# Which engine subtracts the low parts of the down projection's weight blocks: GpSimd or DVE

## The chip, the cores and the metric

One core of one Trainium2 chip runs the whole layer in one launch. The metric is the device time of that launch in microseconds; lower is better. The engines are called as the profile calls them: PE (TensorE), DVE (VectorE), ACT (ScalarE), POOL (GpSimd) and SP, whose queue issues nearly all DMAs.

## The reference, cut to what matters

The layer is a token mixer (Fourier groups and gated DeltaNet heads) followed by a gated convolutional feed-forward, all in float32, for 1024 tokens of width 1024 and a hidden width of 2816. The change lies in the last matrix product of the second part:

```python
def conv_ffn(h, w_up_l, w_dwc_l, w_down_l, on_grid):
    p = h @ w_up_l
    val, gate = p[..., :D_FF], p[..., D_FF:]
    gate = lax.conv_general_dilated(gate.reshape(bsz, rows, GRID_W, D_FF), w_dwc_l[:, :, None, :], ...)
    return (jax.nn.silu(gate) * val) @ w_down_l          # 1024 x 2816 times 2816 x 1024
...
xl = xl + gt2l * rmsnorm(conv_ffn(hl, ...), g_post_ffn[i])
```

## The kernel before, in words

**Split products.** A float32 operand is split into a high part that PE multiplies exactly and a low part that is what is left: high = cast (ACT), low = full minus high (`sub_l`, L164 and L165). `mm3` (L189 to L193) then makes each product of three matmuls: high by high, high by low, low by high. L191 to L193 are the lines of nearly every matmul in the profile, and L165 is the line of every low-part subtraction, whichever engine does it.

**The down projection.** It is the last stage of the kernel (the loop from L1774). The product is cut into 2 x 2 x 2 blocks and done with seven block products instead of eight, so there are seven passes (`PASSES`, L1552), each of 11 steps (`NJ`): 77 steps, numbered n = 0 to 76. A step multiplies four tiles of 128 tokens with one weight block of 128 x 512, which is 4 x 3 = 12 matmuls. A pass collects in four PSUM banks. In passes 0 to 3 either the activations or the weights are a sum of two blocks; in passes 4, 5 and 6 both are.

**What one step needs** is made by `prep(n)` (L1576 to L1608):
- the weight block, one or two DMAs from SP into `raw` (L1589; a page `pg` or, for every fourth step, one of two buffers named `wr`), and for two blocks their sum on DVE (L1591);
- its high part `wh` (cast on ACT, L1598) and its low part `wl` (L1599, shown under L165), each in a ring of four buffers; the last six steps take pages (`pg`) instead;
- the activations: their sum on DVE (L1603, into `s` or one of four halves of `pad`), the cast on ACT (L1606) and the low part on DVE (L1607, shown under L165 as pg<-pad,pg or pg<-pg,pg).

`prep(n + 5)` is written while step n multiplies, so work is prepared up to five steps ahead; the four buffers of `wh` and `wl` let step n's block be split only once PE is done with step n - 4. `raw` is free for its next load when its last reader, the subtraction of `wl`, is done; the DMAs that fill it stand in SP's queue, in order.

```python
nc.scalar.copy(wh, raw[:, 0])
self.sub_l(nc.gpsimd, wl, raw[:, 0], wh)
...
gs = self.page2()
nc.scalar.copy(gs[:, 0], src[0])
self.sub_l(V, gs[:, 1], src[0], gs[:, 0])
```

**What else runs there.** When a pass ends, ACT copies its four banks out (L1804), and small jobs are put into the list `late`, one of which is taken out per step: sums of pass results on POOL (L1808, L1812, L1818, L1820, all shown under L1448), the square and scaling of a finished half (`early`, L1737), and the output of four token tiles (`out`, L1743 to L1757), where DVE does the small norm arithmetic (L201 to L206, L1751) and the last multiply-add (L1756). The last six steps of pass 6 are done tile by tile (L1792), each tile followed by its `out`. The steps 0 to 3 are prepared while the up projection still runs (L1722); DVE is then busy with the taps of the depthwise convolution (L1471), after which ACT applies SiLU (L1475).

The order of the instructions on each engine is fixed when the program is built, by a scheduler that follows the data; each engine then takes its own list strictly in order.

Of the kernel before, what the change touches and what calls it, by code (L numbers as in the profile page):

```python
# [100 lines left out]
class Kern:  # L101
# [1323 lines left out]
    def ffn(self):  # L1425
        nc, tc, A = self.nc, self.tc, self.A
        V = nc.vector
        wu = A["w_up"][0].rearrange("(k p) n -> p k n", p=P)
        with tc.tile_pool(name="ffn", bufs=1, reuse_waits="tile") as fp:
# [134 lines left out]
            def gpart(f, i):  # L1564

                if f not in here:
                    here[f] = [f >= NF - 5] * 2
                    if not here[f][0]:
                        g[f] = self.pg()
                c = slice(512 * i, 512 * i + 512)  # L1570
                if not here[f][i]:
                    nc.sync.dma_start(g[f][:, c], gd[f][:, c])
                    here[f][i] = True
                return g[f][:, c]

            def prep(n):  # L1576

                ps, j = divmod(n, NJ)
                ga, wa = PASSES[ps]
                if ps == 4 and j == 0:  # L1580
                    self.gp2 = self.pg()
                    nc.sync.dma_start(self.gp2, self.gp[1])
                if n % 4:
                    raw = self.pg().rearrange("p (a n) -> p a n", a=2)
                else:
                    raw = self.wp.tile([P, 2, 512], F32, tag="raw", bufs=2, name=self.nm("wr"))
                for x, (k, c, _) in enumerate(wa):
                    f = j + NJ * k
                    nc.sync.dma_start(raw[:, x], A["w_down"][0, f * P:(f + 1) * P, 512 * c:512 * c + 512])  # L1589
                if len(wa) > 1:  # L1590
                    V.tensor_tensor(raw[:, 0], raw[:, 0], raw[:, 1], op=ALU.add if wa[1][2] > 0 else ALU.subtract)  # L1591
                if ps == 6 and j >= NJ - 6:
                    hl = self.page2()
                    wh, wl = hl[:, 0], hl[:, 1]
                else:
                    wh = self.wp.tile([P, 512], F32R, tag="wh", bufs=4, name=self.nm("wh"))
                    wl = self.wp.tile([P, 512], F32R, tag="wl", bufs=4, name=self.nm("wl"))
                nc.scalar.copy(wh, raw[:, 0])  # L1598
                self.sub_l(nc.gpsimd, wl, raw[:, 0], wh)  # L1599
                src = [gpart(j + NJ * k, i) for i, k, _ in ga]  # L1600
                if len(ga) > 1:
                    tmp = big("s") if ps == 0 else tmps[n % 4]
                    V.tensor_tensor(tmp, src[0], src[1], op=ALU.add if ga[1][2] > 0 else ALU.subtract)  # L1603
                    src = [tmp]
# [3 lines that stand above are left out]
                return gs, wh, wl  # L1608
# [74 lines left out]
            for n, (f, p) in enumerate(seq):  # L1683
# [38 lines left out]
                if n >= len(seq) - 4:  # L1722
                    i = len(ops)
                    ops[i] = prep(i)
            work(len(back))
            for i in range(5):
                if i not in ops:
                    ops[i] = prep(i)
# [45 lines left out]
            for ps in range(7):  # L1774
                bk = banks[BSET[ps]]
                for j in range(NJ):
                    n = ps * NJ + j
                    a = 5
                    if ps == 6 and j >= 5:
                        a += j - 5 + 1  # L1780
                    for i in range(n + 5, min(n + a, NS - 1) + 1):
                        if i not in ops:
                            ops[i] = prep(i)
                    if n < NS - 6:
                        for t in range(4):
                            mm(n, t)
                    if late and j > 0 and (ps < 6 or len(late) > 4 or j % 5 == 5 - 1):
                        late.pop(0)()
                    if ps in (5, 6) and j >= NJ - 5 and len(ahead) < 4 * (ps - 4):
                        load_x1(len(ahead))  # L1790
# [69 lines left out]
```

## Time and profile before

| what | value |
| --- | --- |
| time, median of 3 runs | 1411.86 us (1411.44 to 1413.65) |
| time of the profiled execution | 1411.65 us |
| its span, first to last instruction | 1409.9 us |
| mean granted TensorE clock | 0.978 |
| busy share of PE / DVE / ACT / POOL | 92% / 74% / 44% / 48% |
| down projection, from its first matmul | about 1142.6 us to the end |

Times in the profile count from the start of the span. A duration of PE is modelled at its end, so the pace of matmuls is read from the distance between starts. "Idle before" is time in which the engine had nothing to do before the instruction, with the engine and line that ended the wait. On DVE neighbouring instructions overlap by some 0.08 us, so there too the distance between starts is the cost.

### The profile page before, as it was taken

To read this page: it belongs to the slowest core of one execution; us is meant where nothing else is said; L and a number is where in the kernel's file an instruction comes from. 1 tells how busy PE (TensorE), PEld (TensorE's weight loads), DVE (VectorE), ACT (ScalarE), POOL (GpSimd) and SP (SyncE) were. 2 spreads that over 40 slices of the span, in tenths; PEclk is the share of its full clock that TensorE was granted. 3 is DMA by queue.
4 is the path that set the end of the run, shared out by engine and by line. 5 is a ranking of instruction groups with operands and counts; after the bars stand their busy time and mean duration, and the time that the engine had idled before them with its cause. 6 is when DMAs were issued, how large, how long until landed. Compare 5 with 4: busy or idle time off the path is not lost.

```text
span 1409.9 us, 19321 instructions
## 1 busy us (share of the span) xinstructions
PE 1296.7 (92%) x6678; PEld 1028.1 (73%) x6678; DVE 1044.1 (74%) x1715; ACT 614.2 (44%) x1292; POOL 675.5 (48%) x593
## 2 busy tenths in 40 slices
PE   5999999989899999989988999999999989998685
PEld 2677876566566889877866777888888877886564
DVE  3675556836855847865688888888887899799977
ACT  5343456433543234345354344444444445454432
POOL 0440123232351354345365666666666647656773
PEclk9999999999999999999999999999999999999988
DMA  9522237676386778542403133222332285443454
GB/s 326 175 97 82 69 90 219 206 202 210 137 235 226 256 237 268 182 143 86 156 21 87 63 90 90 76 90 75 90 90 75 78 268 192 162 142 122 141 209 179
DMA packets 181427, 209.47 MB, mean 149 GB/s; under 512 B 31383, under 2 KB 119505, under 8 KB 181329
## 3 DMA queue, kind: packets, MB, share of 16 engines
q1 hardware_dynamic: 180465, 205.09, 45.2%
q0 software_dynamic: 864, 3.15, 0.7%
q8 instruction: 53, 0.87, 0.2%
q14 instruction: 45, 0.37, 0.1%
HBM read 161.01 MB, written 47.19 MB: 148 GB/s over the span
## 4 chain that ended last, share of the span: by engine, by line
PE 43%; DVE 17%; DMA 5%; issue 5%; POOL 5%; ACT 3%; SPq 0%; DVEq 0%; ACTq 0%; POOLq 0%
PE ps L191 11%; PE ps L192 11%; PE ps L193 11%; PE ps L1081 3%; POOL wl L165 2%; DVE cv L1471 2%; DVE pg L165 2%; PE ps L1025 1%; DVE T L982 1%; DVE s L1448 1%; POOL pg L165 1%; DVE pg L984 1%; PE ps L305 1%; DVE pg L1756 1%; POOL pg L1006 1%
## 5 line engine op out<-in xcount | busy, mean ns | idle before, releaser
L191 PE MATMUL ps<-pg,wh 128*128 128x512 f32 (+1 forms) x896 | 352.8, 394 | 13.2 <-ACT m L1703 10.0
L193 PE MATMUL ps<-pg,wl 128*128 128x512 f32 (+1 forms) x896 | 348.2, 389 | 0.6 <-POOL wl L165 0.6
L192 PE MATMUL ps<-pg,wh 128*128 128x512 f32 (+1 forms) x896 | 347.6, 388 | 0.0
L1471 DVE SCALAR_TENSOR_TENSOR cv<-pad,dw,cv 128x1024 f32<-128x1024 f32 x176 | 226.4, 1286 | 16.5 <-ACT cv L1469 13.1
L191 PEld LDWEIGHTS ps<-pg,wh 128*128 128x128 f32 x896 | 170.0, 190 | 62.9 <-issue 15.0
L165 POOL TENSOR_TENSOR wl<-wr,wh 128x512 fp32r<-128x512 f32 x86 | 126.2, 1472 | 179.8 <-ACT wh L183 123.7
L193 PEld LDWEIGHTS ps<-pg,wl 128*128 128x128 f32 x896 | 170.7, 190 | 37.1 <-issue 3.5
L192 PEld LDWEIGHTS ps<-pg,wh 128*128 128x128 f32 x896 | 170.7, 190 | 31.2 <-issue 0.4
L165 POOL TENSOR_TENSOR wl<-pg,wh 128x512 fp32r<-128x512 f32 x83 | 124.1, 1499 | 98.7 <-ACT wh L1641 54.1
L165 POOL TENSOR_TENSOR wl<-s,wh 128x512 fp32r<-128x512 f32 x80 | 107.4, 1344 | 54.0 <-ACT wh L1641 53.5
L192 PE MATMUL ps<-wl,pg 128*128 128x512 f32 x250 | 101.7, 407 | 22.0 <-POOL wl L165 21.9
L191 PE MATMUL ps<-wh,pg 128*128 128x512 f32 x250 | 101.0, 405 | 6.2 <-ACT pg L1606 3.5
L1641 ACT CAST wh<-s 128x512 fp32r<-128x512 f32 x80 | 49.6, 621 | 121.5 <-PE ps L192 109.5
L193 PE MATMUL ps<-wh,pg 128*128 128x512 f32 x250 | 99.6, 400 | 0.0
L193 PE MATMUL ps<-pg,pg 128*128 128x512 f32 (+1 forms) x248 | 96.7, 392 | 2.9 <-POOL pg L165 2.1
L191 PE MATMUL ps<-pg,pg 128*128 128x512 f32 (+1 forms) x248 | 97.5, 393 | 0.8 <-DVE pg L476 0.8
L192 PE MATMUL ps<-pg,pg 128*128 128x512 f32 (+1 forms) x248 | 96.4, 389 | 1.4 <-POOL pg L165 1.4
L192 PEld LDWEIGHTS ps<-wl,pg 128*128 128x128 f32 x250 | 48.5, 194 | 35.7 <-POOL wl L165 26.1
L191 PEld LDWEIGHTS ps<-wh,pg 128*128 128x128 f32 x250 | 48.6, 195 | 17.7 <-ACT pg L1606 4.0
L1081 PE MATMUL ps<-pg,pg 128*128 128x128 f32 x464 | 58.4, 277 | 2.7 <-DVE pg L1143 1.8
L1081 PEld LDWEIGHTS ps<-pg,pg 128*128 128x128 f32 x464 | 54.8, 192 | 4.6 <-DVE pg L1143 2.2
L193 PEld LDWEIGHTS ps<-pg,pg 128*128 128x128 f32 x248 | 47.0, 190 | 15.2 <-POOL pg L165 3.6
(363 smaller groups left out, 2540.5 us busy)
## 6 DMA issues: line engine op xcount, KB each, us to landing
pg<-in_w_down_dram SPq DMA_DIRECT2D x97, 256.0 KB, 4.5
wr<-in_w_ada_dram SPq DMA_DIRECT2D x32, 512.0 KB, 4.4
wr<-in_w_up_dram SPq DMA_DIRECT2D x24, 512.0 KB, 3.8
wr<-in_w_in_dram SPq DMA_DIRECT2D x20, 512.0 KB, 4.7
pg<-in_w_up_dram SPq DMA_DIRECT2D x20, 512.0 KB, 5.9
wr<-in_w_down_dram SPq DMA_DIRECT2D x35, 256.0 KB, 2.7
gd<-pg SPq DMA_DIRECT2D x17, 512.0 KB, 2.6
pg<-gd SPq DMA_DIRECT2D x34, 256.0 KB, 4.2
```

The lines of the kernel that those rows point to most:

```text
L165: eng.tensor_tensor(l, full, h.bitcast(F32), op=ALU.subtract)
L191: nc.tensor.matmul(out, ah, bh, start=start, stop=False, **kw)
L192: nc.tensor.matmul(out, ah, bl, start=False, stop=False, **kw)
L193: nc.tensor.matmul(out, al, bh, start=False, stop=stop, **kw)
L305: nc.tensor.matmul(ps[32 * j:32 * j + 32, :], self.csil[:, k, :], t[:, a, :], start=(k < 4), stop=(k >= 4), skip_group_check=True, tile_po ...
L982: V.tensor_tensor(tmp, L[:nl, j + 1:, j:j + 1].broadcast_to([nl, r, c]), X[:nl, j:j + 1, 0:c].broadcast_to([nl, r, c]), op=ALU.mult)
L984: V.tensor_tensor(X[:nl, j + 1:, 0:c], X[:nl, j + 1:, 0:c], tmp, op=ALU.subtract)
L1006: nc.gpsimd.tensor_tensor(dst[:, d].rearrange("p h (b c) -> p h b c", b=4), src.unsqueeze(2).broadcast_to([P, H, 4, 32]), mask, op=ALU.mult)
L1025: nc.tensor.matmul(ps[po, h * n:(h + 1) * n], Q[k0:k0 + kn, d, h, po], R[k0:k0 + kn, d, h, c0:c0 + n], start=True, stop=True, skip_group_c ...
L1081: nc.tensor.matmul(ps[:, hs(h)], lhs(h), rhs(h), start=True, stop=True, skip_group_check=True)
L1471: V.scalar_tensor_tensor(c3, src, w, c3, op0=ALU.mult, op1=ALU.add)
L1641: nc.scalar.copy(h, src)
```

## The change

The low part of each of the 77 weight blocks of the down projection is subtracted by DVE. Operands, buffers and loads stay as they are.

```diff
--- before.py
+++ after.py
@@ -1596,7 +1596,7 @@
                     wh = self.wp.tile([P, 512], F32R, tag="wh", bufs=4, name=self.nm("wh"))
                     wl = self.wp.tile([P, 512], F32R, tag="wl", bufs=4, name=self.nm("wl"))
                 nc.scalar.copy(wh, raw[:, 0])
-                self.sub_l(nc.gpsimd, wl, raw[:, 0], wh)
+                self.sub_l(V, wl, raw[:, 0], wh)
                 src = [gpart(j + NJ * k, i) for i, k, _ in ga]
                 if len(ga) > 1:
                     tmp = big("s") if ps == 0 else tmps[n % 4]
```

It changes the lists of two engines most: DVE has 1506 entries instead of 1429, POOL 485 instead of 563 (an entry can stand for two equal instructions in a row).

DVE in pass 5, before, around the weight sums of steps 60 and 58 (`wr_11409` and `pg_11355`); L165 here is the low part of activations only:

```order
L1603 TENSOR_TENSOR pad_6493<-pg_9438 128x512
L165 TENSOR_TENSOR pg_11364<-pad_6494,pg_11364 128x512
L1591 TENSOR_TENSOR wr_11409<-wr_11409 128x512
L165 TENSOR_TENSOR pg_11388<-pad_6494,pg_11388 128x512
L1591 TENSOR_TENSOR pg_11355<-pg_11355 128x512
L1603 TENSOR_TENSOR pad_6494<-pg_9590 128x512
L1603 TENSOR_TENSOR pad_6494<-pg_9742 128x512
```

DVE at the same place with the change; `wl_11256` and `wl_11282` are weight low parts of steps 54 and 55:

```order
L165 TENSOR_TENSOR pg_11364<-pad_6494,pg_11364 128x512
L1603 TENSOR_TENSOR pad_6494<-pg_9932 128x512
L165 TENSOR_TENSOR wl_11256<-pg_11251,wh_11255 128x512
L1591 TENSOR_TENSOR pg_11355<-pg_11355 128x512
L165 TENSOR_TENSOR pg_11388<-pad_6494,pg_11388 128x512
L1591 TENSOR_TENSOR wr_11409<-wr_11409 128x512
L165 TENSOR_TENSOR wl_11282<-pg_11277,wh_11281 128x512
L1591 TENSOR_TENSOR pg_11379<-pg_11379 128x512
```

One weight subtraction now stands in each step's share of the list, between the sums for later steps, and those sums wait behind it.

POOL in pass 5 before, from the sums of pass results on:

```order
L1448 TENSOR_TENSOR pg_11403<-pg_11403,pg_10586 128x512 x2
L1448 TENSOR_TENSOR pg_11404<-pg_11404,pg_10587 128x512
L165 TENSOR_TENSOR wl_11360<-pg_11355,wh_11359 128x512
L1448 TENSOR_TENSOR pg_11404<-pg_11404,pg_10587 128x512
L165 TENSOR_TENSOR wl_11384<-pg_11379,wh_11383 128x512
L165 TENSOR_TENSOR wl_11414<-wr_11409,wh_11413 128x512
L165 TENSOR_TENSOR wl_11438<-pg_11433,wh_11437 128x512
```

POOL at the same place with the change:

```order
L1448 TENSOR_TENSOR pg_11403<-pg_11403,pg_10586 128x512 x2
L1448 TENSOR_TENSOR pg_11404<-pg_11404,pg_10587 128x512 x2
L1448 TENSOR_TENSOR pg_11403<-pg_11403,pg_10995 128x512 x2
L1448 TENSOR_TENSOR pg_11404<-pg_11404,pg_10995 128x512
L1448 TENSOR_TENSOR pg_11125<-pg_11125,pg_10995 128x512
```

Only the sums of pass results and the scalings of the output are left on POOL there.

DVE at the start of the stage with the change, in the last taps of the convolution (L1471); the four `wl` are those of steps 1 to 4:

```order
L165 TENSOR_TENSOR wl_9978<-pg_9975,wh_9977 128x512
L1471 SCALAR_TENSOR_TENSOR cv<-pad_6494,dw,cv 128x1024
L165 TENSOR_TENSOR wl_10010<-pg_10007,wh_10009 128x512
L1471 SCALAR_TENSOR_TENSOR cv<-pad_6494,dw,cv 128x1024
L165 TENSOR_TENSOR wl_10035<-pg_10032,wh_10034 128x512
L1471 SCALAR_TENSOR_TENSOR cv<-pad_6494,dw,cv 128x1024
L165 TENSOR_TENSOR pg_10040<-s_10038,pg_10040 128x512
L1471 SCALAR_TENSOR_TENSOR cv<-pad_6494,dw,cv 128x1024
L165 TENSOR_TENSOR wl_10053<-wr_10050,wh_10052 128x512
L1471 SCALAR_TENSOR_TENSOR cv<-pad_6494,dw,cv 128x1024
```

Before, these taps stand with the activations' sums and subtractions alone; the first of the five early weight subtractions, that of step 0, now stands some ten entries further ahead.

## Rows read from the trace of the kernel before

**Rows 1.** Busy time, share of the span and instructions, from the page.
```profile
PE 1296.7 (92%) x6678; PEld 1028.1 (73%) x6678; DVE 1044.1 (74%) x1715; ACT 614.2 (44%) x1292; POOL 675.5 (48%) x593
```

**Rows 2.** Stretches of the down projection: busy time (count) by engine, granted clock.
```profile
core 0: us, PE busy (x) PEld busy (x) DVE busy (x) ACT busy (x) POOL busy (x), PEclk, DMA share, GB/s
1142.50:1170.00 27.50, 22.24 (x90) 17.50 (x89) 26.30 (x30) 13.01 (x24) 15.34 (x8) 0.94 0.66 224
1170.00:1274.00 104.00, 104.00 (x460) 86.11 (x460) 91.38 (x82) 53.33 (x100) 66.79 (x45) 1.00 0.52 169
1274.00:1383.90 109.90, 85.54 (x336) 65.66 (x334) 98.03 (x113) 40.72 (x80) 77.58 (x45) 0.91 0.43 146
1383.90:1409.90 26.00, 12.76 (x55) 10.25 (x55) 20.03 (x48) 4.41 (x15) 7.09 (x5) 0.79 0.59 212
1249.40:1383.90 134.50, 110.14 (x444) 86.05 (x442) 119.76 (x133) 51.70 (x98) 91.81 (x54) 0.92 0.45 153
```

**Rows 3.** Timeline of PE: start, duration, what, idle before and its releaser.
```profile
1159.95 0.80 PE L191 MATMUL ps<-wh,pg 128*128 128x512 f32 x1 [3.53 <-ACT pg L1606]
1166.73 0.50 PE L192 MATMUL ps<-wl,pg 128*128 128x512 f32 x1 [1.73 <-POOL wl L165]
...
1177.31 0.39 PE L191 MATMUL ps<-wh,pg 128*128 128x512 f32 x1
...
1180.03 0.39 PE L191 MATMUL ps<-wh,pg 128*128 128x512 f32 x1
...
1341.08 0.80 PE L192 MATMUL ps<-wl,pg 128*128 128x512 f32 x1 [9.08 <-POOL wl L165]
```

**Rows 4.** PE's waits from 1170 to 1384: for whom, us in total, times, longest.
```profile
PE ps L192 <- POOL wl L165: 20.2, 7, 9.1
PE ps L191 <- ACT wh L1598: 2.6, 1, 2.6
PE ps L192 <- POOL pg L165: 0.7, 2, 0.4
PE ps L193 <- DVE pg L165: 0.7, 1, 0.7
```

**Rows 5.** Timeline of DVE in passes 5 and 6.
```profile
1311.18 1.78 DVE L1591 TENSOR_TENSOR wr<-wr 128x512 f32<-128x512 f32 x1
...
1333.20 0.69 DVE L1603 TENSOR_TENSOR pad<-pg 128x512 f32<-128x512 f32 x1
1333.80 0.69 DVE L1591 TENSOR_TENSOR pg<-pg 128x512 f32<-128x512 f32 x1
...
1348.43 0.69 DVE L1591 TENSOR_TENSOR pg<-pg 128x512 f32<-128x512 f32 x1 [8.52 <-DMA pg<-in_w_down_dram]
...
1383.18 0.68 DVE L165 TENSOR_TENSOR pg<-pad,pg 128x512 fp32r<-128x512 f32 x1
```

**Rows 6.** Timeline of POOL in pass 5.
```profile
1312.38 1.74 POOL L165 TENSOR_TENSOR wl<-wr,wh 128x512 fp32r<-128x512 f32 x1
...
1331.59 9.44 POOL L165 TENSOR_TENSOR wl<-wr,wh 128x512 fp32r<-128x512 f32 x1 [5.60 <-DVE pg L1591]
...
1346.12 1.29 POOL L165 TENSOR_TENSOR wl<-wr,wh 128x512 fp32r<-128x512 f32 x1 [1.40 <-ACT wh L1598]
```

**Rows 7.** The chain that ended last, in order of time, in passes 5 and 6.
```profile
1335.10 5.94 POOL wl L165
...
1344.33 7.94 DMA pg<-in_w_down_dram
```

**Rows 8.** Groups of POOL's instructions, 1249.3 to 1383.9: busy, mean ns, idle before.
```profile
L165 POOL TENSOR_TENSOR wl<-pg,wh 128x512 fp32r<-128x512 f32 x25 | 38.3, 1536 | 16.3 <-ACT wh L1598 15.2 <-issue 1.1
L165 POOL TENSOR_TENSOR wl<-wr,wh 128x512 fp32r<-128x512 f32 x8 | 21.0, 2628 | 12.6 <-ACT wh L1598 5.7 <-DVE pg L1591 5.6 <-issue 1.3
```

**Rows 9.** Groups of DVE's instructions, the same stretch: a small one.
```profile
L203 DVE RECIPROCAL sums<-rsq 128x1 f32<-128x1 f32 x3 | 0.4, 149 | 0.0
```

**Rows 10.** Timeline of ACT at the start of the stage.
```profile
1158.37 1.02 ACT L1475 ACTIVATE pg<-cv 128x1024 f32<-128x1024 f32 x1 [9.45 <-DVE cv L1471]
```

## The prediction

> **What bounds the kernel now.** PE is busy for 92% of the span [rows 1], an average over stages with different limits, so I read the last stage by stretches [rows 2]. First its floor: twelve matmuls, one step, take 1180.03 - 1177.31 = 2.72 us from start to start, 0.227 us each [rows 3]. From 1170 to 1274 (passes 0 to 3) PE is busy all the time at a granted clock of 1.00 [rows 2]: nothing on another engine can shorten that stretch. From 1274 to 1383.9 (passes 4 to 6) 336 matmuls, worth 336 x 0.227 = 76.3 us, take 109.9 us at a clock of 0.91 [rows 2]: 33.6 us are lost. The waits of PE account for 20.2 + 2.6 + 0.7 + 0.7 = 24.2 us of them, 20.2 for POOL's subtraction of `wl`, the instruction that is moved [rows 4]; the other 9.4 us go with the lower clock after such pauses.
>
> Who is late behind POOL? DVE is busy for 119.8 of the 134.5 us from 1249.4, where it takes up the first weight sum of pass 4, to 1383.9, where its last subtraction for the last step ends [rows 2, 5]. But most of that is not its work. Next to each other stand full-size DVE instructions (128x512, two inputs in SBUF) that cost 0.60 us from start to start and others that take 1.78 us; the long ones lie beside a POOL subtraction that takes 1.74 us where an undisturbed one takes 1.29 [rows 5, 6]. The two engines stand in each other's way, by about 1.78 - 0.68 = 1.10 us for DVE at a meeting. Once it goes the other way: a POOL subtraction that starts at 1331.59 ends 9.44 us later, while DVE runs one 0.69 us instruction after another [rows 5, 6]. PE waits 9.08 us for it [rows 3]; its raw buffer comes free late, the chain goes on through the next load (5.94 us of POOL, then 7.94 us of DMA), and DVE then stands idle for 8.52 us [rows 5, 7].
>
> The Trainium skill says of this ("SBUF — State Buffer", section "Who interferes with whom") that a DVE instruction with two SBUF inputs and a GpSimd instruction that reads SBUF take the shared port for a whole instruction each, and that whichever issues second waits until the first finishes. The 1.78 us rows agree [rows 5]; the 9.44 us row does not, since POOL was held for (9.44 - 1.29) / 0.60, some 13, DVE instructions, not one [rows 5, 6]. By the page alone the 8.5 us term below would not be the port's and would stay.
>
> **The change part by part.**
>
> *POOL loses 77 subtractions.* In the stretch from 1249.4, POOL has 54 instructions; 25 + 8 = 33 are subtractions into the `wl` ring [rows 2, 8], and six more are those of the last six steps, so 39 leave and 15 sums and scalings stay. What did the 54 cost DVE? Of its 133 instructions 115 are full-size and 18 of the small norm kind; at 0.61 and 0.15 us [rows 5, 9] they are worth 70.2 + 2.7 = 72.9 us, so 119.8 - 72.9 = 46.9 us are time in POOL's way, 0.87 us for each POOL instruction. Taking 39 away is worth 39 x 0.87 = 33.9 us.
>
> *DVE gets 39 of the 77 in that stretch*, with the same shape as those it has: 39 x 0.61 = 23.8 us. DVE's busy time falls by 33.9 - 23.8 = **10.1 us**.
>
> *The late load goes.* With no `wl` on POOL none can be held up, so the chain that ended in 8.5 us of DVE idleness has no start: **8.5 us**. The other 134.5 - 119.8 - 8.5 = 6.2 us of idle time in the stretch I leave in. The next late thing is DVE itself: its 119.8 - 10.1 = 109.7 us of work for passes 4 to 6 still exceed PE's 33 x 2.72 = 89.8 us, so PE goes on waiting for it now and then.
>
> *Passes 0 to 3.* DVE gets one more 0.61 us instruction per step, with POOL gone from its way. PE has no wait there [rows 2] and a step has 2.72 us for DVE's three; cost 0. If that cover went (a `wl` standing behind a late load in DVE's list), each 2.72 us that DVE stands still beyond the three steps that are prepared would be one step of PE.
>
> *The start.* Five weight subtractions now stand among DVE's last taps, ahead of the SiLU that ACT waits for and behind which the casts for step 4 stand; ACT waits 9.45 us for those taps [rows 10] and PE 3.53 us for the cast [rows 3]. Cost at most 5 x 0.61 = 3.1 us. Against it, three other full-size DVE instructions (two of L1603, one of L1591) move behind the taps in DVE's list, POOL is out of the way, and the 1.73 us that PE waits for `wl` of a later step [rows 3] can go too: gain at most 3.5 + 1.7 = 5.2 us. I take 0, since additions and removals are nearly equal in number.
>
> *SP's queue* issues the same loads; those into `raw` are released by the subtraction on DVE instead of POOL. I cost this at nothing because the subtraction is shorter, and keep the other case as a rival.
>
> *The tail.* From DVE's last subtraction to the end lie 26 us, mostly 55 matmuls and DVE's final multiply-adds [rows 2]. POOL's scalings there stay. The tail moves as a whole; cost 0.
>
> Sum, against the profiled execution's own 1411.65 us (0.2 us under the median of the three runs): 1411.65 - 10.1 - 8.5 = **1393.0 us**. The ends: PE without any loss from 1274 on, and the best start, give 1411.65 - 33.6 - 5.2 = 1372.9 us; only the 10.1 us and the worst start give 1411.65 - 10.1 + 3.1 = 1404.7 us. I stay near the middle, because the ledger of DVE is made of many equal rows, while the floor supposes that DVE is never late again.
>
> **The rivals.**
>
> *PE's floor is reached.* If DVE, freed of POOL, also starts passes 4 to 6 with more work done ahead, all 33.6 us come back: 1378.1 us. For it: DVE's 115 + 39 = 154 full-size instructions at the undisturbed 0.61 us are 93.9 us, hardly more than PE's 89.8. Against it: 15 POOL instructions remain, worth 13 us of DVE by the same 0.87.
>
> *Hidden anyway: the loads set the pace.* If the 8.5 us of idleness and more of its kind come from late loads whoever frees the buffers, DVE's 10.1 us turn into idle time: about 1411.7 us, no change. Against it: the long wait begins at the held-up subtraction [rows 7], and PE's waits are for `wl`, not for DMA [rows 4]. That the change does not do what it says is excluded by DVE's 77 new entries.
>
> *DVE inherits POOL's waits; slower.* POOL waited 15.2 + 5.7 = 20.9 us for ACT's `wh` in that stretch [rows 8], partly because the ring is full until PE finishes a step. On POOL nothing stood behind that wait; in DVE's list the sums and subtractions for later steps do. If DVE stands still as long and the load chain stays, the time is 1411.65 - 10.1 + 20.9 = 1422.5 us. It decides from the point where the inherited waits exceed 10.1 us, or 18.6 us if the load chain goes. Against it: the ring is full only while PE is behind, and from 1274 on it is PE that waits [rows 4].
>
> *DVE is simply full; slower.* If POOL's presence is not what makes the 1.78 us rows, the 39 subtractions only add: 1411.65 + 23.8 = 1435.5 us. Against it: wherever POOL is held up or idle, DVE's rows are 0.69 us [rows 5]. The Trainium skill's page "Perfetto Trace Analysis" (section "Optimizing Scalar/DVE Operations") advises moving work away from a saturated DVE, even to GpSimd, and adds that shifting it between these two might not help as they share a read port; by its first half this rival would hold, and the 0.60 us starts speak for its second.
>
> **How the numbers follow.** Forecast 0.64, PE's floor 0.19, no change 0.07, inherited waits 0.06, a full DVE 0.04. Faster by over 0.2% (2.8 us, about what a measurement of this kernel can tell from no change): 0.64 + 0.19 = 0.83; within it 0.07; slower 0.06 + 0.04 = 0.10. The predicted time is the forecast's, 1393.0 us. The range holds the forecast and the floor with their bounds, from 1374 (the last microsecond of the best start left out) to 1407 us (2 us past the weaker end, towards no change), and leaves out some 0.19.
>
> **What would show it.** In the profile after: DVE's full-size instructions in passes 4 to 6 mostly at 0.6 to 0.7 us, with some 15 meetings left; no PE wait for a POOL line in the steps; DVE's last subtraction near 1365 us; passes 0 to 3 still without a wait of PE; the clock above 0.91. Wrong would be a DVE that waits for ACT's `wh` or for loads with `wl` behind it, PE waiting in passes 0 to 3, or 1.78 us rows where POOL does nothing.

## The result, and the profile after

| | before | after |
| --- | --- | --- |
| time, median (range), 4 runs each (one of before added) | 1411.65 us (1407.52 to 1413.65) | 1390.46 us (1386.4 to 1395.8) |
| time of the profiled execution, its span | 1411.65 us, 1409.9 us | 1392.15 us, 1390.3 us |
| ratio, 95% interval | | 0.9858 [0.9827, 0.9889] |

The change saves 1.4%, 20.0 us of 1411.65 by the ratio. The forecast was 1393.0 us, faster.

The page first: busy time of each engine, its share of the span, its instructions.

```profile
PE 1297.3 (93%) x6673; PEld 1032.7 (74%) x6678; DVE 1019.5 (73%) x1792; ACT 614.6 (44%) x1292; POOL 547.0 (39%) x516
```

DVE has 77 instructions more than before [rows 1] and is busy 24.6 us less. The stretches of the down projection show where that lies. The second begins and ends where the same work does in [rows 2]: 1247.60 is the first weight sum of pass 4, 1365.20 the end of DVE's last subtraction for the last step.

```profile
core 0: us, PE busy (x) PEld busy (x) DVE busy (x) ACT busy (x) POOL busy (x), PEclk, DMA share, GB/s
1170.00:1274.30 104.30, 104.30 (x461) 86.37 (x461) 82.31 (x128) 55.87 (x105) 7.94 (x6) 1.00 0.54 179
...
1247.60:1365.20 117.60, 108.44 (x453) 87.90 (x452) 108.92 (x171) 52.24 (x100) 24.92 (x15) 0.95 0.52 177
...
1274.30:1365.20 90.90, 81.74 (x335) 65.78 (x334) 87.87 (x139) 38.96 (x77) 22.96 (x14) 0.94 0.51 177
1365.20:1390.30 25.10, 13.24 (x53) 10.45 (x51) 19.17 (x48) 4.42 (x15) 7.10 (x5) 0.77 0.61 220
```

Read against [rows 2]: passes 0 to 3 are as they were, PE busy all the time at a clock of 1.00. From 1274.3 on, 335 matmuls at 0.227 us [rows 3] are worth 76.0 of 90.9 us: 14.9 us are lost where 33.6 were, and the clock is 0.94 where it was 0.91. The stretch from pass 4's first sum to DVE's last subtraction shrinks from 134.5 to 117.6 us, by 16.9; it begins 1.8 us earlier, and the tail is 0.9 us shorter. 16.9 + 1.8 + 0.9 = 19.6 us is the whole difference of the spans, 1409.9 - 1390.3.

What is left of PE's waits of over half a microsecond, from the start of the stage on (timeline of PE: start, duration, what, idle before and its releaser):

```profile
1160.25 0.80 PE L191 MATMUL ps<-wh,pg 128*128 128x512 f32 x1 [3.06 <-ACT pg L1606]
...
1291.95 0.50 PE L192 MATMUL ps<-wl,pg 128*128 128x512 f32 x1 [3.20 <-DVE wl L165]
1314.11 0.79 PE L192 MATMUL ps<-wl,pg 128*128 128x512 f32 x1 [3.94 <-DVE wl L165]
...
1362.56 0.51 PE L191 MATMUL ps<-pg,pg 128*128 128x512 f32 x1 [1.94 <-ACT pg L1606]
```

The 9.08 us wait of before and the 1.73 us wait at the start [rows 3] are gone, and no wait of PE here is for POOL. The last three make 9.1 of the 14.9 us; the other 5.7 us are longer matmuls (busy for 81.7 us instead of 76.0), at the clock of 0.94. The two waits for DVE's `wl` stand right behind sums of pass results that POOL still does. This is the first of them on DVE, with POOL's rows at that time:

```profile
1284.27 0.68 DVE L165 TENSOR_TENSOR pg<-pad,pg 128x512 fp32r<-128x512 f32 x1
1286.15 1.78 DVE L1448 TENSOR_TENSOR s<-s,pg 128x512 f32<-128x512 f32 x1 [1.21 <-POOL pg L1448]
1287.85 1.77 DVE L1591 TENSOR_TENSOR wr<-wr 128x512 f32<-128x512 f32 x1
1289.55 1.75 DVE L1603 TENSOR_TENSOR pad<-pg 128x512 f32<-128x512 f32 x1
1291.22 0.68 DVE L165 TENSOR_TENSOR wl<-pg,wh 128x512 fp32r<-128x512 f32 x1
```

```profile
1283.88 3.50 POOL L1448 TENSOR_TENSOR pg<-s,m 128x512 f32<-128x512 f32 x2 [4.90 <-issue]
1287.35 3.40 POOL L1448 TENSOR_TENSOR pg<-pg,pg 128x512 f32<-128x512 f32 x2
```

DVE has three rows of 1.75 to 1.78 us in a line while POOL works through its sums, and rows of 0.68 us before and behind; the `wl` for which PE waits comes right after. Over the whole stretch DVE's subtraction of `wl` is nearly undisturbed (groups: count, busy, mean ns, idle before), and its last subtraction stands where the forecast put it, near 1365:

```profile
L165 DVE TENSOR_TENSOR wl<-pg,wh 128x512 fp32r<-128x512 f32 x25 | 18.7, 748 | 1.5 <-ACT wh L1598 1.4
```

```profile
1364.50 0.68 DVE L165 TENSOR_TENSOR pg<-pad,pg 128x512 fp32r<-128x512 f32 x1
```

### The profile page after: what moved, and what is told of

Same layout as the page of the kernel before. It is cut to its first block, busy times and chain, and to the rows that moved or that the text cites. A ratio compares the mean times of both kernels' runs of the same rounds, so it can differ in the third digit from the quotient of the medians.

```text
span 1390.3 us, 19234 instructions
## 1 busy us (share of the span) xinstructions
PE 1297.3 (93%) x6673; PEld 1032.7 (74%) x6678; DVE 1019.5 (73%) x1792; ACT 614.6 (44%) x1292; POOL 547.0 (39%) x516
## 4 chain that ended last, share of the span: by engine, by line
PE 41%; DVE 19%; DMA 6%; issue 6%; POOL 4%; ACT 2%; SPq 1%; DVEq 0%; POOLq 0%; ACTq 0%
PE ps L191 11%; PE ps L193 11%; PE ps L192 11%; DVE cv L1471 3%; PE ps L1081 2%; DVE pg L165 2%; DVE s L1448 2%; PE ps L1025 1%; DVE T L982 1%; DMA pg<-in_w_down_dram 1%; DVE pg L984 1%; DVE wl L165 1%; POOL wl L165 1%; POOL pg L165 1%; PE ps L305 1%
## 5 line engine op out<-in xcount | busy, mean ns | idle before, releaser
L191 PE MATMUL ps<-pg,wh 128*128 128x512 f32 (+1 forms) x896 | 353.1, 394 | 12.8 <-ACT m L1703 10.1
L1471 DVE SCALAR_TENSOR_TENSOR cv<-pad,dw,cv 128x1024 f32<-128x1024 f32 x176 | 226.3, 1286 | 16.5 <-ACT cv L1469 13.1
L165 POOL TENSOR_TENSOR wl<-wr,wh 128x512 fp32r<-128x512 f32 x68 | 89.7, 1326 | 161.4 <-ACT wh L183 128.6
L165 POOL TENSOR_TENSOR wl<-s,wh 128x512 fp32r<-128x512 f32 x80 | 108.1, 1352 | 56.0 <-ACT wh L1641 55.4
L191 PE MATMUL ps<-pg,pg 128*128 128x512 f32 (+1 forms) x248 | 99.0, 400 | 2.7 <-ACT pg L1606 1.9
L193 PE MATMUL ps<-pg,pg 128*128 128x512 f32 (+1 forms) x248 | 97.9, 398 | 2.3 <-POOL pg L165 2.1
L192 PE MATMUL ps<-pg,pg 128*128 128x512 f32 (+1 forms) x248 | 97.9, 395 | 0.7 <-POOL pg L165 0.7
L1448 POOL TENSOR_TENSOR pg<-pg,pg 128x512 f32<-128x512 f32 x20 | 31.4, 1586 | 139.9 <-ACT pg L1804 81.7
L165 POOL TENSOR_TENSOR wl<-pg,wh 128x512 fp32r<-128x512 f32 x30 | 39.7, 1323 | 55.5 <-ACT wh L1641 55.5
L191 PEld LDWEIGHTS ps<-pg,pg 128*128 128x128 f32 x248 | 48.0, 194 | 14.8 <-ACT pg L1606 2.2
L193 PEld LDWEIGHTS ps<-pg,pg 128*128 128x128 f32 x248 | 47.9, 193 | 14.8 <-POOL pg L165 3.6
```

The source lines that it names most:

```text
L165: eng.tensor_tensor(l, full, h.bitcast(F32), op=ALU.subtract)
L191: nc.tensor.matmul(out, ah, bh, start=start, stop=False, **kw)
L192: nc.tensor.matmul(out, ah, bl, start=False, stop=False, **kw)
L193: nc.tensor.matmul(out, al, bh, start=False, stop=stop, **kw)
L1448: eng.tensor_tensor(o, a, b, op=op)
L1471: V.scalar_tensor_tensor(c3, src, w, c3, op0=ALU.mult, op1=ALU.add)
```

## The experiments

**Where the gain lies.** Two kernels move the weight subtraction in one part of the passes only, 33 steps and 44 steps.

```diff
-                self.sub_l(nc.gpsimd, wl, raw[:, 0], wh)
+                self.sub_l(V if n >= 4 * NJ else nc.gpsimd, wl, raw[:, 0], wh)
```

> The weight blocks' low parts go to DVE in passes 4 to 6 only (steps 44 to 76); POOL keeps those of passes 0 to 3. Port theory (POOL's subtractions lengthen DVE's instructions, and that matters only where DVE sets the pace): the whole gain stays, 1390 us within 4 us. Rival, start theory (the gain comes from the first steps and the extra lead that passes 0 to 3 give): most of it goes, 1400 us or more.

Measured: 1393.75 us (1392.06 to 1396.41) against 1411.33, ratio 0.9876 [0.9847, 0.9905], so 17.5 us less.

```diff
-                self.sub_l(nc.gpsimd, wl, raw[:, 0], wh)
+                self.sub_l(V if n < 4 * NJ else nc.gpsimd, wl, raw[:, 0], wh)
```

> The converse: DVE takes them in passes 0 to 3 only (steps 0 to 43), POOL keeps those of passes 4 to 6. Port theory: no gain, 1411 us within 4 us, since PE has no wait in passes 0 to 3 and DVE's rows in passes 4 to 6 are long again. Start theory: 1395 us or less.

Measured: 1407.82 us (1405.79 to 1410.96), ratio 0.9974 [0.9956, 0.9992], so 3.7 us less. In its trace PE still waits for POOL in passes 4 to 6 as before, 9.09 us at the longest, while its wait for a `wl` at the start is gone:

```profile
PE ps L192 <- POOL wl L165: 19.2, 7, 9.1
```

What follows: 17.5 us of the gain belong to passes 4 to 6 and some 4 us to the start of the stage (from 1170 to 1274 PE is busy all the time in the second kernel too, so nothing is gained there). Together they are 21.2 us, where the full change gives 20.0.

**POOL's presence, or its late result?** To the changed kernel, 33 POOL subtractions of the same size were added in passes 4 to 6. They write a tile that nobody reads, so no engine waits for what they write.

```diff
                 self.sub_l(V, gs[:, 1], src[0], gs[:, 0])
+                if n >= 4 * NJ:
+                    idle = fp.tile([P, 512], BF16, tag="idle", bufs=1, name=self.nm("idle"))
+                    self.sub_l(nc.gpsimd, idle, gs[:, 1].bitcast(F32), gs[:, 0])
```

> The changed kernel, and from step 44 on POOL also subtracts the high from the low part of each step's activations, into a scratch tile of bfloat16 that nobody reads: 33 further POOL instructions with two inputs in SBUF; nothing that PE or DVE waits for is added. Port theory: each costs DVE about 0.87 us, DVE's full-size rows of 1.7 us come back, and the time rises by 20 to 30 us, to 1410 to 1420 us. Rival, late-result theory (what cost time before was that PE and the loads waited for POOL's results; the long DVE rows filled idle time): no change, 1390 us within 4 us.

Measured: 1421.45 us (1416.35 to 1425.3), ratio 1.0068 [1.0046, 1.0089]: slower than before, (1.0068 - 0.9858) x 1411 = 30 us over the change, and a little above the 1410 to 1420 us expected. The stretch, PE's waits and a group of DVE:

```profile
1247.60:1396.50 148.90, 116.93 (x454) 89.25 (x454) 144.21 (x171) 52.21 (x101) 76.98 (x47) 0.92 0.42 141
```

```profile
PE ps L192 <- DVE wl L165: 26.0, 16, 5.4
```

```profile
L165 DVE TENSOR_TENSOR wl<-pg,wh 128x512 fp32r<-128x512 f32 x25 | 29.7, 1189 | 1.3 <-ACT wh L1598 1.3
```

DVE has the same 171 instructions as in the change and needs 144.21 us for them in place of 108.92; the same subtraction takes 1189 ns on the mean in place of 748. PE has no wait for POOL at all, and loses 26.0 us behind DVE. DVE doesn't wait for POOL either: its idle time in the stretch is 148.9 - 144.21 = 4.7 us, less than the 117.6 - 108.92 = 8.7 us with the change. POOL's mere presence is the cost.

**The price of a meeting, by itself.** A small kernel sets the two engines against each other.

> Leaves out the whole layer: bursts of 128x512 float32 subtractions only. In order: 8 on DVE alone; 8 on POOL alone; 16 on DVE and 6 on POOL let go by the same cast; 6 on POOL with 12 on DVE let go when POOL's first is done; 8 on POOL with 8 on DVE of which each waits for an ACT cast of the one before; 16 on DVE with the second input in PSUM and 6 on POOL. Port theory: alone 0.60 us from start to start on DVE and 1.3 us on POOL; in the third burst one engine holds the other out or they take turns at 1.7 us; in the fourth and fifth they take turns; in the sixth both keep their undisturbed pace, since DVE has one SBUF input. Rival (SBUF bandwidth is shared): both slow down in every common burst, the sixth too, by the same factor throughout.

The phases on DVE, and the same on POOL (alone; both let go together; POOL first; second input in PSUM):

```profile
4.82 4.90 DVE L26 TENSOR_TENSOR dv<-x,y 128x512 f32<-128x512 f32 x8 [4.82 <-ACT y L35]
20.94 16.11 DVE L26 TENSOR_TENSOR dv<-x,y 128x512 f32<-128x512 f32 x16 [11.22 <-ACT y L35]
39.08 12.61 DVE L26 TENSOR_TENSOR dv<-x,po 128x512 f32<-128x512 f32 x12 [2.03 <-POOL po L26]
...
73.32 9.65 DVE L26 TENSOR_TENSOR dv<-x,q 128x512 f32<-128x512 f32 x16 [2.57 <-ACT x L34]
```

```profile
10.46 9.80 POOL L26 TENSOR_TENSOR po<-x,y 128x512 f32<-128x512 f32 x8 [10.01 <-ACT x L34]
20.99 10.10 POOL L26 TENSOR_TENSOR po<-x,y 128x512 f32<-128x512 f32 x6 [0.73 <-ACT y L35]
37.78 9.15 POOL L26 TENSOR_TENSOR po<-x,y 128x512 f32<-128x512 f32 x6 [6.70 <-ACT x L34]
...
73.43 7.41 POOL L26 TENSOR_TENSOR po<-x,y 128x512 f32<-128x512 f32 x6 [9.35 <-ACT x L34]
```

Alone DVE needs 4.90 / 8 = 0.61 us and POOL 9.80 / 8 = 1.22 us. Let go together they take turns: 16 of DVE last 16.11 us, 16.11 - 16 x 0.61 = 6.35 more, which is 1.06 us for each of POOL's six, and POOL's own last 1.68 us. With DVE's second input in PSUM neither notices the other (0.60 and 1.24 us). In the fifth phase, which isn't shown, DVE waited for a cast each time; its three rows wholly beside POOL were 0.99 us, its last four, without POOL, 0.69: where DVE pauses anyway, a meeting cost it 0.30 us.

**Why one subtraction was held for 9.44 us [rows 6].** The turns above don't explain it. The first test:

> A small kernel that leaves out the whole layer and writes another output: DVE runs 20 subtractions (128x512, two SBUF inputs) without a pause; one or four POOL subtractions are let go by ACT's cast of DVE's third result. In order: 1 POOL; 4 POOL; 1 POOL while DVE's are a chain in which each reads the one before; 1 POOL and then 4 POOL while each of DVE's reads a tile of its own that ACT wrote. Theory 'held out' (a POOL instruction that arrives while DVE runs back to back waits until DVE pauses, as the 9.44 us row suggests): the single POOL row lasts 8 to 11 us, until DVE's last, and DVE's rows stay at 0.6 to 0.7 us. Theory 'turns' (as in the bursts that start together): the single POOL row lasts 1.7 us, and one DVE row beside it lasts 1.7 us. If it depends on DVE's instructions waiting for nothing, the phases differ: held out in the first, turns in the chain.

POOL's rows, phase by phase; the last is the first of the four of the fifth phase:

```profile
7.59 1.59 POOL L26 TENSOR_TENSOR po<-c,y 128x512 f32<-128x512 f32 x1 [7.15 <-ACT c L63]
21.46 6.59 POOL L26 TENSOR_TENSOR po<-c,y 128x512 f32<-128x512 f32 x4 [12.28 <-ACT c L63]
38.84 1.78 POOL L26 TENSOR_TENSOR po<-c,y 128x512 f32<-128x512 f32 x1 [10.79 <-ACT c L63]
65.17 1.60 POOL L26 TENSOR_TENSOR po<-c,y 128x512 f32<-128x512 f32 x1 [24.54 <-ACT c L63]
...
78.28 10.62 POOL L26 TENSOR_TENSOR po<-c,y 128x512 f32<-128x512 f32 x1 [11.51 <-ACT c L63]
```

Neither theory holds for all: four phases took turns, chain or not, and the fifth was held, although its instructions are those of the fourth. What differs is that in the fifth phase DVE had run on from the fourth, over 20 instructions without a pause. That became the next experiment, where only the moment of POOL's arrival changes.

> A small kernel that leaves out the whole layer: eleven runs of 26 subtractions on DVE (128x512, two SBUF inputs) without a pause, each begun after a wait; in each, one POOL subtraction is let go by ACT's cast of DVE's result number 1, 3, 4, 5, 6, 7, 9 or 12. Then three runs with number 9 in which DVE meets something else: at number 8 a wait for a cast of ACT, at number 16 an instruction that reads PSUM, at number 16 one of 128x1. Theory 'a long run shuts POOL out' (in the kernel before, POOL arrived after nine undisturbed DVE instructions and was held for 9.44 us; in the small kernel before this, after four, it took its turn, and after 23 it was held): the POOL row lasts 1.6 us up to some number between 4 and 9, and from there on until DVE's last, 10 us or more; after the wait at number 8 it takes its turn again; the PSUM instruction at 16 lets it in (row near 5 us) or not; the 128x1 one likewise. Rival (it hangs on which data the instructions read, or on chance in the arrival): no such threshold, the rows of the first eight runs alike or mixed.

DVE's runs with POOL let go by result 4 and 5, and the places with the PSUM and the 128x1 instruction; then POOL's rows for result 4, 5 and 12, behind the wait, and in the last two runs:

```profile
39.63 16.81 DVE L26 TENSOR_TENSOR dv<-x,y 128x512 f32<-128x512 f32 x26 [0.69 <-ACT x L34]
57.12 15.74 DVE L26 TENSOR_TENSOR dv<-x,y 128x512 f32<-128x512 f32 x26 [0.69 <-ACT x L34]
...
174.75 0.68 DVE L26 TENSOR_TENSOR dv<-pb,y 128x512 f32<-128x512 f32 x1
...
191.64 1.23 DVE L26 TENSOR_TENSOR sm<-x,y 128x1 f32<-128x1 f32 x1
```

```profile
42.99 1.47 POOL L26 TENSOR_TENSOR po<-c,y 128x512 f32<-128x512 f32 x1 [16.62 <-ACT c L78]
61.07 12.91 POOL L26 TENSOR_TENSOR po<-c,y 128x512 f32<-128x512 f32 x1 [16.62 <-ACT c L78]
...
137.55 8.70 POOL L26 TENSOR_TENSOR po<-c,y 128x512 f32<-128x512 f32 x1 [9.37 <-ACT c L78]
154.58 1.47 POOL L26 TENSOR_TENSOR po<-c,y 128x512 f32<-128x512 f32 x1 [8.34 <-ACT c L78]
172.07 3.88 POOL L26 TENSOR_TENSOR po<-c,y 128x512 f32<-128x512 f32 x1 [16.02 <-ACT c L78]
188.96 3.89 POOL L26 TENSOR_TENSOR po<-c,y 128x512 f32<-128x512 f32 x1 [13.00 <-ACT c L78]
```

The border lies between two neighbouring cases. Arriving 42.99 - 39.63 = 3.36 us after DVE's run began, POOL gets its turn; arriving 61.07 - 57.12 = 3.95 us after, it is shut out until the run ends (57.12 + 15.74 = 72.86; POOL's row ends at 73.98), and so in all the later cases. Whether time or the number of DVE's instructions decides, these runs don't tell apart, since DVE's rows are alike. A pause of DVE for a cast starts the count anew (POOL arrives at 154.58, 7.13 us after DVE began but 2.14 us after its pause, and has its turn); an instruction that reads PSUM lets POOL in at once (it ends 1.20 us after 174.75), and so does one of 128x1, which then takes 1.23 us itself. In the kernel before, POOL arrived at 1331.59, and DVE's run of 0.69 us rows had begun at 1326.46, 5.13 us earlier: past the border. DVE paid nothing for the shut-out: its run of 26 lasts 15.74 us, 16.81 with a turn in it.

Two limits of this. POOL instructions that follow each other without a gap keep their turns however long DVE runs (the six in the burst of 16.11 us). And how short a pause is enough is open: with the change a POOL sum arrives at 1306.33, 10.09 us after DVE's last wait ended at 1296.24, and has its turn at once; 2.1 us ahead of it DVE's rows leave a gap of 0.06 us (1304.15 to 1304.21). No run tests whether that gap let it in.

**Is it the held instruction, or any?** In the kernel before, only the subtractions that read `wr`, one of which was held, were moved, nine of the 33.

```diff
-                self.sub_l(nc.gpsimd, wl, raw[:, 0], wh)
+                self.sub_l(V if n >= 4 * NJ and n % 4 == 0 else nc.gpsimd, wl, raw[:, 0], wh)
```

> The kernel before, with only the weight subtraction of every fourth step of passes 4 to 6 (steps 44, 48 to 76, nine of 33; those that read wr) moved to DVE. Theory A (the late load was its own term of 8.5 us and hangs on the wr subtraction that was held up for 9.44 us): 9 x (0.87 - 0.61) = 2.3 us plus 8.5 us, so 10 to 11 us less than before, near 1401 us, no POOL row over 4 us. Theory B (any POOL subtraction can be held up, and the idle time of DVE goes only as POOL's share goes): 2 to 6 us less than before, 1405 to 1409 us, with another POOL row of 5 us or more and a PE wait behind it.

Measured: 1406.85 us (1403.41 to 1411.01) against 1411.07, ratio 0.9968 [0.9954, 0.9982], 4.5 us less by the ratio. Another subtraction is held in the same place, 1332.46 - 1326.20 = 6.26 us after DVE's run there began:

```profile
1332.46 9.53 POOL L165 TENSOR_TENSOR wl<-pg,wh 128x512 fp32r<-128x512 f32 x1 [8.48 <-DVE pg L165]
```

Behind it PE waits 3.12 us for `wl`, but DVE only 0.69 us for a load (at 1341.56), not 8.52. Its idle time from the first weight sum of pass 4 to its last subtraction hardly falls all the same: 130.07 - 117.27 = 12.8 us where it was 14.7, because it now waits 6.9 us for loads into `wr`, none of them behind the hold. As theory B has it, the gain goes with the number moved, 4.5 / 9 = 0.50 us each, close to the 17.5 us / 33 = 0.53 of the first experiment.

**The shut-out taken away alone.** The kernel before, with a small DVE instruction as a break behind each activation sum:

```diff
                     V.tensor_tensor(tmp, src[0], src[1], op=ALU.add if ga[1][2] > 0 else ALU.subtract)
+                    if n >= 4 * NJ:
+                        brk = fp.tile([P, 1], F32, tag="brk", bufs=1, name=self.nm("brk"))
+                        V.tensor_tensor(brk, tmp[:, 0:1], tmp[:, 1:2], op=ALU.add)
                     src = [tmp]
```

> The kernel before, with a DVE instruction of 128x1 (two SBUF inputs, a sum that nobody reads) written behind each activation sum of passes 4 to 6, 33 of them; they come after 1 to 7 full-size ones in DVE's list. In the small kernel such an instruction let a POOL subtraction in that had been shut out. The weight subtractions stay on POOL, so this takes away the shutting out alone. Theory (the late load begins with the shut-out and costs its own 6 to 9 us): no POOL row over 4 us, no PE wait of 9 us near 1340, 3 to 9 us less than before. Rival (being shut out only defers a meeting; DVE pays 0.9 to 1.1 us for each POOL instruction then or later, and the load is late anyway): the long row goes, and the time stays within 3 us of before, or rises by the 33 breaks of 0.1 to 1.2 us.

Measured: 1411.38 us (1406.28 to 1414.56) against 1410.0, ratio 0.9998 [0.9983, 1.0014]: no change. The stretch from the first weight sum of pass 4, in this trace at 1254.35, to DVE's last subtraction; the breaks; PE's waits for `wl` from 1171 on, behind those of the start:

```profile
1254.35:1386.80 132.45, 111.07 (x438) 85.70 (x436) 126.64 (x165) 51.35 (x98) 90.59 (x53) 0.93 0.46 155
```

```profile
L1606 DVE TENSOR_TENSOR brk<-pad 128x1 f32<-128x1 f32 x33 | 22.1, 671 | 0.4
```

```profile
PE ps L192 <- POOL wl L165: 18.2, 9, 4.9
```

The 9 us wait is gone, and PE loses 18.2 us in nine smaller ones where it lost 20.2 us in seven [rows 4]. DVE's wait for the late load is gone too: its idle time in the stretch falls from 134.5 - 119.76 = 14.7 us to 132.45 - 126.64 = 5.8 us, but its busy time rises by 6.9. Of the 33 breaks 17 last 0.15 us; in the other 16 POOL has its turn, and they last 1.1 to 1.3 us. Reckoned as in the prediction, DVE's own work in the stretch, with 32 breaks at 0.15 us, is 115 x 0.61 + 50 x 0.15 = 77.7 us, and 126.64 - 77.7 = 48.9 us are time in POOL's way where it was 46.9: 0.92 us for each of 53 instructions. This is what the rival expects: while POOL was shut out, DVE ran some 13 instructions without a meeting and then waited; without the shut-out it has the meetings instead. But the 33 breaks' own time, some 5 us at 0.15 us each, could hide a gain of about that size, so a smaller cost of the hold itself is not excluded.

**A version that beats both.** The rest of POOL's work in the down projection goes to DVE: sixteen sums of pass results and eight scalings of the output; fifteen of these 24 stand in the stretch of passes 4 to 6.

```diff
-                tt((V, nc.gpsimd)[3 >> hf & 1], src[1], src[1], self.gp2[:, cs[1]], ALU.mult)
+                tt(V, src[1], src[1], self.gp2[:, cs[1]], ALU.mult)
...
-                        late.append(lambda t=t: tt(nc.gpsimd, M["M4"][t], M["M4"][t], M["M5"][t], ALU.subtract))
+                        late.append(lambda t=t: tt(V, M["M4"][t], M["M4"][t], M["M5"][t], ALU.subtract))
```

and the same at L1812, L1818 and L1820.

> The changed kernel with the last GpSimd work of the down projection moved to DVE too: the sums of pass results and the scaling in the output; POOL does nothing there any more. Theory (GpSimd's presence costs DVE more than the work itself): the 15 POOL instructions of passes 4 to 6 go, 15 x (0.87 - 0.61) = 3.9 us, and the two PE gaps of 3.2 and 3.9 us that stand right behind POOL's pairs at 1285 and 1308 us go as well: between 4 and 11 us faster than the changed kernel, so 1380 to 1387 us where that shows 1390.5; no full-size DVE row over 0.8 us after 1250. Rival (DVE is now the bound by its own work, its rows add up): 15 x 0.61 = 9.2 us more of DVE plus up to 5 us in the tail, so 1395 to 1405 us. The sums of passes 2 to 3, which also move, cost nothing in either.

Measured: 1379.53 us (1379.26 to 1383.09) against 1411.07, ratio 0.9784 [0.9762, 0.9806], apart from the change's [0.9827, 0.9889] and 10 us below it. The stretches (the first again from the first weight sum of pass 4 to DVE's last subtraction), PE's waits from 1170 to 1360, and DVE's group:

```profile
1245.90:1355.25 109.35, 107.89 (x474) 88.41 (x473) 104.34 (x185) 52.77 (x100) 0.00 (x0) 1.00 0.56 188
1274.00:1355.30 81.30, 79.83 (x350) 65.18 (x350) 80.67 (x149) 37.90 (x71) 0.00 (x0) 1.00 0.58 197
1355.30:1377.70 22.40, 6.65 (x30) 5.17 (x28) 17.43 (x53) 4.63 (x15) 0.00 (x0) 0.69 0.67 247
```

```profile
PE ps L191 <- ACT pg L1606: 1.4, 1, 1.4
```

```profile
L165 DVE TENSOR_TENSOR wl<-pg,wh 128x512 fp32r<-128x512 f32 x25 | 17.1, 685 | 1.0 <-ACT wh L1598 1.0
```

DVE does 14 more instructions in the stretch than with the change and is busy 4.6 us less; its 104.34 us are what 167 x 0.61 + 18 x 0.15 = 104.6 us of undisturbed work come to, so nothing is left of POOL's way. The waits of 3.20 and 3.94 us are gone, and PE runs at a granted clock of 1.00 to DVE's last subtraction. This is about the floor of PE that the prediction reckoned at 1378.1 us, though the tail, 22.4 us in place of 25.1, is shorter as well.

## Why the prediction was right, and where it was not

**POOL's way, -33.9 + 23.8 = -10.1 us: right, and for the reason given.** DVE's busy time in the stretch fell from 119.76 to 108.92 us, by 10.8. The price of 0.87 us for each POOL instruction, worked out from the ledger of before, comes out again from that of after: (108.92 - 153 x 0.61 - 18 x 0.15) / 15 = 0.86 us. In the kernel with added POOL work the same sum gives (144.21 - 153 x 0.61 - 18 x 0.15) / 47 = 1.03 us, in that with breaks 0.92, and the small kernel 1.06. So the price is not fixed, and it doesn't go by how many there are: 54 cost 0.87 us each, 47 cost 1.03. It is highest where DVE has least idle time in the stretch (14.7 us before, 8.7 with the change, 5.8 with the breaks, 4.7 with the added work). A likely reason is that fewer of them fall into a pause of DVE, as in the small kernel's fifth phase; no run of the whole kernel tests it.

**The late load, -8.5 us: 6.1 measured, and not borne out as a term of its own.** DVE's idle time fell from 14.7 to 8.7 us, by 6.1 where the sum had 8.5. The step said that this chain starts at the held-up subtraction and goes with it. In one place it was misread: the load of 7.94 us [rows 7] ends at 1344.33 + 7.94 = 1352.27, after DVE had gone on at 1348.43 [rows 5], so it isn't the one for which DVE stood idle. What ties the two together is SP's queue. Its next load, into `wr`, was issued when the held subtraction ended (1331.59 + 9.44 = 1341.03), after 17.5 us of waiting, and other loads stood in line behind it:

```profile
1341.06 0.33 SPq L1589 DMA_DIRECT2D wr<-in_w_down_dram  x1
```

Taking the hold away alone left the time within [0.9983, 1.0014] (the kernel with breaks), and with the held kind of instruction moved another was held, the long wait for the load was gone, and only 4.5 us were gained. This speaks for the 8.5 us of waiting being mostly the other side of meetings that DVE had been spared, so that the two terms are largely one: what DVE loses to 54 POOL instructions, met or waited out. It is not shown to the last microsecond, since the breaks leave a cost of the hold itself of up to some 5 us open. That the gain goes with the number moved (0.50 and 0.53 us each) speaks for one cause too. Why 6.1 us of idle time went beside the 10.8 us of busy time, and not more or less, is not settled. That the forecast came so close has some luck in it: 10.8 + 6.1 = 16.9 us stand against 18.6 in the sum, and 1.8 us at the start and 0.9 us in the tail, both put at 0, made up for it.

**The start, 0: it gave a little.** The bounds were -5.2 to +3.1. With the change in passes 0 to 3 alone the time fell by 3.7 us (1.1 to 6.2 by the interval), of which PE's 1.73 us wait and 3.53 - 3.06 = 0.47 us of the other [rows 3] are seen.

**Passes 0 to 3, SP's queue and the tail, 0 each: right to within a microsecond.** PE is busy all of 104.3 us there, the tail is 25.1 us where it was 26.0, and DVE waits 2.1 + 1.5 us for loads in the stretch, the 8.52 us wait [rows 5] being gone. DVE does wait for ACT's `wh` with `wl` in its own list, the mechanism of the slower rival, but 2.1 us in the stretch, not the 20.9 of POOL:

```profile
DVE pg L1591 <- DMA pg<-in_w_down_dram: 2.1, 2, 1.3
DVE wl L165 <- ACT wh L1598: 2.1, 3, 0.7
DVE wr L1591 <- DMA wr<-in_w_down_dram: 1.5, 2, 1.2
```

**The rivals.** PE's floor was not reached by the change, because of POOL's 15 remaining instructions, as the prediction had it; without them it is. "Hidden anyway" would have been 1411.7 us, "DVE simply full" 1435.5. The Trainium skill's page "Perfetto Trace Analysis", section "Optimizing Scalar/DVE Operations", was its support: a saturated DVE may hand work to GpSimd, with the reservation that the two share a read port. The runs go with the reservation, and past it: each full-size instruction on POOL took 0.86 to 1.06 us of DVE's time, more than the 0.61 us for which DVE does it itself.

**The hold.** The prediction set the 9.44 us row against the Trainium skill's page "SBUF — State Buffer", section "Who interferes with whom", by which the one that issues second waits until the first one's instruction is done. The turns of 1.7 us agree, and so does the Trainium skill's rule there that a DVE instruction with at most one SBUF input, outside the two-port modes, doesn't contend (the PSUM phase, 0.60 and 1.24 us). The hold of up to 12.91 us does not: there the measurement decides.

## What to carry to other kernels

Before work goes to GpSimd to relieve DVE, price it in DVE's time: read DVE's rows with and without a POOL row beside them, and compare the difference times POOL's count with what DVE would need itself. Here an instruction of 128x512 with two SBUF inputs cost DVE more time on POOL than on DVE itself, down to the last 15 of the stretch, whose move gave another 10 us. And a long wait that ends the chain need not be a cost of its own: take it away alone before counting it.

## What the runs showed of the hardware that was not expected

- A POOL instruction that arrives over some 3.4 to 4.0 us into an unbroken run of undisturbed DVE instructions of 128x512 with two SBUF inputs is shut out until the run pauses (12.91 us in the small kernel, 9.44 us in the kernel before); an earlier one takes its turn (1.5 to 1.8 us). A wait of DVE (0.68 us), an instruction of 128x1 or one that reads PSUM lets it in. Why the border lies there, and how short a pause is enough, no run shows.
- Being shut out costs DVE nothing (15.74 us for 26 instructions); a turn costs it 1.07 us (16.81).
